# Moving HBM weight sums behind attention and retention, with a new issue order, in a hybrid decoder block

## The chip, the cores and the metric

The kernel runs on one core of a Trainium2 chip. The metric is the device time of one execution in microseconds, and lower is better. A core has TensorE (PE, matrix products and transposes), VectorE (DVE), ScalarE (ACT), GpSimd (POOL) and SyncE (SP). Every engine works through its own list of instructions in order, so an instruction that waits holds up all that stand behind it on that engine. SP issues nearly all loads and stores; POOL issues the transfers that add in HBM.

## The reference

One decoder layer, batch 1, 512 positions, width 1024, float32. The two mixers share one input projection; a gated sum of them goes through one output projection.

```python
h = rms_norm(x, norm_pre)
(q_n, k_c, v_c, k_s, v_s, k_w, v_w, g_n, z_n,
 q_r, k_r, v_r, z_r, m_a, m_b) = jnp.split(h @ w_in, split_points(), axis=-1)
# mixer A: 8 query heads of 64, 2 key groups; three branches, each with its own sigmoid gate
#   compressed keys (windows of 32, step 16, a two-layer gelu net), selected blocks, sliding window
o = g[..., 0:1] * o_c + g[..., 1:2] * o_s + g[..., 2:3] * o_w
y_a = (o * silu(z_n)) @ w_nsa_o
# mixer B: retention in chunks of 128, 4 heads, key width 128, value width 256
o_b = group_norm(o_inner + o_cross)
y_b = (o_b * silu(z_r)) @ w_ret_o
merged = sigmoid(m_a) * y_a + sigmoid(m_b) * y_b
x = x + rms_norm(merged @ w_out, norm_post)
```

With 512 positions the 16 "best" of 8 blocks are all blocks and the window covers every earlier position, so the selected and the sliding branch are both causal attention, on their own keys and values.

## The kernel before, in words

**Three products for one.** Each float32 matrix is held as a high part and a low remainder (hTh and hTl, whi and wlo), and a product is high x high + high x low + low x high, all summed in one PSUM bank (mm3). A weight tile comes by SP into one of NR = 4 raw buffers of 128x1024 words (512 KB); ACT or DVE copies it to the high part, DVE subtracts to get the low part (splitter, split_lo), and the parts lie in one of nine pairs of tiles until PE has used them. A few more pairs (more_tiles) come free in the course of the kernel; fits(p) says which pieces of weights may use them: MORE and MORE2 are ranges of load numbers.

**Stages.** PE's main line is in main(): first block A (attention keys and values, PE starts while h is still being made), C, Q; then the blocks of PLAN: Z (mixer A's output gate), MA0, ZR0, QK0, VR0, PAIR, VR1, MB0, NO0, RO0, MA1, NO1, MB1, RO1, and out_seven at the end. Z, MA and MB are the gates, QK, VR and ZR belong to retention (two halves of two heads), NO and RO are the two output matrices. Beside that line run the hidden layer of the compressed branch (hidden, its weights are 8 loads in the stream, HFIRST of which come ahead of Z's), 24 groups of attention (att_head, att_unit, att_block, att_cmp; att_sum ends one of the 8 pieces (t, g), in the order t = 3, 2, 1, 0) and 8 steps of retention (ret(hp, t), one per weight block row of VR).

**Seven products for eight.** PAIR, MA1, MB1 and out_seven are done as 2x2 block products with seven block products in place of eight (Strassen-Winograd's form). Such a product needs sums of blocks of its weights, and some of its inputs. The sums of weights are made in HBM: POOL issues 128x2048-word transfers (1 MB) that write a block to a scratch tensor, and others that add another block to it (accum_op=OP.add). The list seq has 8 transfers for PAIR (tensors pair, here p0 to p7), 8 for MA1 and MB1 together (t, s0 to s7), 8 for out_seven (out, o0 to o7), and three sums H0, H1, H2 of pieces of h (tensors s) that stand at the places HS of the list. In each group the first four write and the last four add. p4 needs p0, p5 needs p1, p6 needs p2 and p5, p7 needs p6 and p3; s and o are alike. H0, H1, H2 need the small stores of h by SP (signed). POOL waits for the landing of what a transfer needs before it issues it.

**Where the sums stand.** add_sums(n) issues the next n of the list. weight_sums issues FIRST = 8 once h is stored, and 27 - FIRST - sum(OSUMS) = 17 once the first tile of Z's gate is there (a POOL copy to a one-word tile named mark carries that wait). ret(hp, t) issues OSUMS[4*hp + t] more, right behind POOL's pow of that step. The finished sums are loaded by SP like other weights (load_next, the branch with DMA.dma_start(raw, o)); that load waits for the sum.

**The order of the work.** All these steps are generators. The class Order plays them at build time: it keeps a clock for PE and for each engine, yields give the time at which a step's input is ready, and of the steps that are ready (ready time + LAG + margin not after the clock) the one with the lowest priority number is issued next; with none, the earliest. PRIOS and MARGINS hold the priorities and the allowances (ns) by name of a generator, OWN those of single instances (split_lo.8 is the ninth split_lo that is spawned, which is the first of block C's). Order.dma models a load: a queue, 353 bytes per ns alone, slow (79 or 142) bytes per ns while a sum is in flight, and 1750 ns + BESIDE (if beside a sum) until it has landed. What comes out is only the order of the instructions on each engine; on the chip each waits for its true inputs.

**Others that the change touches.** EARLY_OUT lists the steps of retention whose PSUM bank is copied out by ACT before it is split. SKEW gives, for a block of weights, how many of its row pieces one output tile takes before the other tile of the pair takes its turn. HOLD_C is an allowance (ns) before the transposes of block C's keys.

Of the kernel before, what the change touches and what calls it, by code (L numbers as in the profile page):

```python
# [18 lines left out]
P = 128  # L19
# [16 lines left out]
MARGINS = {'att_cmp': 100.0, 'att_head': 150.0, 'att_out': 400.0, 'att_sum': 20.0, 'att_unit': 250.0, 'compress': 0.0, 'ga_split': 0.0, 'gates': 800.0, 'h_sums': 400.0, 'hidden': 800.0, 'keep': 0.0, 'kept': 1700.0, 'qk_end': 1700.0, 'ret': 20.0, 'ret_state': 150.0, 'rot_table': 400.0, 's_early': 50.0, 's_late': 150.0, 'seven_end': 0.0, 'split_lo': 150.0, 'splitter': 400.0, 'tail_a': 150.0, 'tail_c': 100.0, 'tail_m': 100.0, 'tail_o': 400.0, 'tail_p': 400.0, 'tail_q': 0.0, 'tail_qk': 600.0, 'tail_yb': 0.0, 'tail_z': 1300.0, 'x_split': 600.0, 'zr_end': 20.0}  # L36
# [7 lines left out]
HOLD_C = 1600  # L44
EARLY = 1300
HOLD = 2000
OSUMS = (1, 0, 0, 0, 1, 0, 0, 0)
FIRST, BESIDE = 8, 2500.0
HS = (4, 7, 9)
DVE_BIAS = 700  # L50
PRIOS = {'att_block': 0, 'att_cmp': 2, 'att_head': 3, 'att_out': 0, 'att_sum': 5, 'att_unit': 3, 'attention': 0, 'compress': 1, 'edges': 3, 'flip': 2, 'ga_split': 2, 'gates': 0, 'h_low': 1, 'h_split': 1, 'h_sums': 3, 'hidden': 3, 'keep': 5, 'kept': 0, 'more_tiles': 1, 'norms': 1, 'qk_end': 0, 'ret': 1, 'ret_state': 1, 'rot_table': 2, 's_early': 1, 's_late': 5, 'seven_end': 0, 'tail_a': 0, 'tail_c': 2, 'tail_m': 0, 'tail_o': 3, 'tail_p': 5, 'tail_q': 3, 'tail_qk': 0, 'tail_ya': 1, 'tail_yb': 3, 'tail_z': 0, 'tail_zr': 1, 'weight_sums': 0, 'x_split': 2, 'zr_end': 2}
OWN = {'edges.0': (5, 2200.0), 'gates.0': (None, 1700.0), 'h_low.0': (None, 100.0), 'h_low.4': (0, None), 'h_low.5': (None, 600.0), 'h_low.6': (1, None), 'more_tiles.0': (0, 150.0), 'norms.0': (None, 20.0), 'qk_end.2': (5, None), 'rot_table.5': (None, 2200.0), 'rot_table.6': (None, 250.0), 'signed.0': (2, 600.0), 'signed.1': (None, 0.0), 'signed.2': (0, 1300.0), 'signed.5': (None, 20.0), 'signed.7': (2, None), 'split_lo.0': (None, 800.0), 'split_lo.1': (None, 1000.0), 'split_lo.101': (4, None), 'split_lo.105': (1, None), 'split_lo.11': (3, None), 'split_lo.111': (None, 800.0), 'split_lo.13': (None, 600.0), 'split_lo.15': (2, 20.0), 'split_lo.19': (None, 400.0), 'split_lo.2': (0, None), 'split_lo.6': (2, None), 'split_lo.8': (4, 1300.0), 'split_lo.9': (None, 50.0), 'tail_a.0': (0, None), 'tail_a.2': (None, 400.0), 'tail_a.3': (0, 0.0), 'tail_c.1': (0, 20.0), 'tail_c.3': (1, None), 'tail_q.1': (1, 20.0), 'tail_qk.4': (None, 600.0), 'tail_qk.5': (None, 600.0), 'weight_sums.0': (0, 1000.0), 'x_split.0': (None, 20.0), 'zr_end.3': (1, None)}
HFIRST, HWANT = 1, 1
MORE, MORE2 = range(12, 24), range(24, 28)
EARLY_OUT = ((0, 3), (1, 0), (1, 3))
SKEW = {'Q': 4}
# [3 lines left out]
class Order:  # L60
# [47 lines left out]
    def dma(self, nbytes, r=0.0, n=1):  # L108
        for _ in range(n):
            self.ring = max(self.ring, r + LAG, self.flying.pop(0) + LAG) + 475  # L110
            t, left, beside = max(self.eng["dma"], self.ring + 100), nbytes / n, False
            slow = 79.0 if left <= P * 2048 else 142.0
            for i, (a, b) in enumerate(self.busy):
                if b <= t or left < 1:
                    continue
                free = min(left, max(0.0, a - t) * 353.0)
                left, t = left - free, t + free / 353.0
                if left >= 1:
                    part = min(left, (b - t) * slow)
                    left, t, beside = left - part, t + part / slow, True  # L120
# [2004 lines left out]
```

## Time and profile before

| | us |
|---|---|
| three runs | 483.2, 486.62, 487.13 |
| median | 486.62 |
| profiled execution, its own time | 486.01 |
| profiled execution, span of its instructions | 484.2 |
| PE busy in it | 469.9 (97%) |
| DVE, ACT, POOL busy in it | 410.4, 332.9, 37.7 |
| POOL's transfers (queue q0), share of 16 engines over the span | 22.8% |
| SP's transfers (queue q1), the same share | 43.2% |

The profiled execution's own time is 1.81 us above its span: that part lies outside the instructions. The median of the three runs is 0.61 us above the profiled one. A matmul's record is longer than the step from one to the next, because they are pipelined: the time between two starts is what one costs. Where a row says "<- ACT words L253", the instruction stood idle until that engine's instruction gave its signal. L301, L265, L253 and L278 are lines of helpers that many steps share, so the tiles' names tell what a row is: whi and wlo are split weights, arena_r holds keys, queries, values and block C's weights, bank is PSUM, words holds most float32 work, raw is a weight tile as it was loaded.

### The profile page before, as it was taken

The numbers are of one execution on the slowest core, as the hardware profiler recorded it, in microseconds if no ns is written. First come the engines' busy times: TensorE is split into PE (matmuls) and PEld (weight loads), VectorE is DVE, ScalarE is ACT, GpSimd is POOL, SyncE is SP. The second block draws the span as 40 slices with busy tenths as digits, with TensorE's granted clock in tenths as the row PEclk, the third lists the DMA queues.
The fourth block names the chain that finished last, engine by engine and source line by source line (L and its number), as shares of the span: only waits on it lengthen the run. The fifth ranks groups of instructions, "written<-read, shape, count | busy, mean of one in ns | idle before, by whom it ended". The sixth has DMA issues, their size and how long they took to land.

```text
span 484.2 us, 7839 instructions
## 1 busy us (share of the span) xinstructions
PE 469.9 (97%) x2676; PEld 419.7 (87%) x2676; DVE 410.4 (85%) x932; ACT 332.9 (69%) x717; POOL 37.7 (8%) x62
## 2 busy tenths in 40 slices
PE   8989999899999999999999999999999999999993
PEld 7879888788888888888989888998889989988882
DVE  5579899988898979889799998977776968989786
ACT  6787689679788899895687687765435435438742
POOL 2103020120002100000110001000000000000000
PEclk9999999999999999999999999999999999999997
DMA  8947999999968994125577662631474736626814
GB/s 307 398 139 252 352 324 272 292 275 396 286 149 199 361 190 129 68 85 177 111 231 263 216 207 83 134 128 40 141 256 151 226 102 200 222 100 214 249 70 164
DMA packets 31080, 98.75 MB, mean 204 GB/s; under 512 B 3136, under 2 KB 6976, under 8 KB 30272
## 3 DMA queue, kind: packets, MB, share of 16 engines
q1 hardware_dynamic: 24576, 70.85, 43.2%
q0 software_dynamic: 6320, 27.26, 22.8%
q8 instruction: 21, 0.34, 0.3%
q10 hardware_dynamic: 144, 0.14, 0.2%
q14 instruction: 19, 0.16, 0.1%
HBM read 93.52 MB, written 31.98 MB: 259 GB/s over the span
## 4 chain that ended last, share of the span: by engine, by line
PE 82%; DMA 6%; DVE 6%; ACT 5%; issue 1%; DVEq 0%; ACTq 0%; SPq 0%
PE bank L301 68%; PE bank L1342 8%; DMA raw<-in_stream_dram 4%; PE bank L307 4%; PE bank L1858 2%; ACT words L253 2%; DVE arena_r L265 2%; DVE words L265 2%; DMA words<-in_rope_r_dram 1%; DVE words L278 1%; ACT rsrow L253 1%; DMA words<-in_x_dram 1%; ACT whi L253 1%; ACT arena_r L253 1%; DVE wlo L265 1%
## 5 line engine op out<-in xcount | busy, mean ns | idle before, releaser
L253 ACT ACTIVATE whi<-raw 128x512 fp32r<-128x512 f32 x170 | 102.2, 627 | 47.5 <-PE bank L301 34.5
L265 DVE TENSOR_TENSOR wlo<-raw,whi 128x512 fp32r<-128x512 f32 x178 | 116.3, 686 | 6.4 <-ACT whi L253 4.8
L301 PE MATMUL bank<-whi,hTh 128*128 128x512 f32 x192 | 72.3, 398 | 1.2 <-ACT words L253 1.0
L301 PE MATMUL bank<-wlo,hTh 128*128 128x512 f32 x192 | 68.9, 379 | 0.0
L301 PE MATMUL bank<-whi,hTl 128*128 128x512 f32 x192 | 68.8, 379 | 0.0
L301 PE MATMUL bank<-arena_r 128*128 128x256 f32 (+2 forms) x328 | 66.6, 324 | 0.0
L301 PE MATMUL bank<-arena_r,whi 128*128 128x512 f32 (+1 forms) x208 | 61.4, 371 | 0.0
L253 ACT ACTIVATE arena_r<-bank 128x512 fp32r<-128x512 f32 (+3 forms) x86 | 45.6, 536 | 21.1 <-PE bank L307 20.5
L253 ACT ACTIVATE words<-words,stat 128x512 f32<-128x512 f32 (+3 forms) x108 | 56.6, 559 | 0.3 <-DVE stat L1071 0.2
L301 PEld LDWEIGHTS bank<-arena_r 128*128 128x128 f32 x328 | 50.9, 190 | 4.4 <-DVE arena_r L265 0.2
L265 DVE TENSOR_TENSOR arena_r<-bank,arena_r 128x512 fp32r<-128x512 f32 (+2 forms) x72 | 46.8, 655 | 5.8 <-ACT arena_r L253 5.1
L301 PEld LDWEIGHTS bank<-arena_r,whi 128*128 128x128 f32 x208 | 39.2, 189 | 5.0
L301 PE MATMUL bank<-hTh,whi 128*128 128x512 f32 (+1 forms) x124 | 43.1, 348 | 0.0
L301 PE MATMUL bank<-hTh,wlo 128*128 128x512 f32 (+1 forms) x124 | 42.0, 339 | 0.0
L301 PE MATMUL bank<-hTl,whi 128*128 128x512 f32 (+1 forms) x124 | 42.0, 339 | 0.0
L301 PEld LDWEIGHTS bank<-whi,hTh 128*128 128x128 f32 x192 | 36.7, 192 | 5.8 <-ACT words L253 1.5
L301 PEld LDWEIGHTS bank<-whi,hTl 128*128 128x128 f32 x192 | 36.4, 190 | 5.3
L301 PEld LDWEIGHTS bank<-wlo,hTh 128*128 128x128 f32 x192 | 36.4, 189 | 3.8
L307 PEld LDWEIGHTS bank<-identr,shorts 128*128 128x128 f32 x276 | 30.7, 141 | 7.9 <-ACT words L253 1.4
L301 PE MATMUL bank<-arena_r,wlo 128*128 128x512 f32 x96 | 36.4, 379 | 0.0
L253 ACT ACTIVATE words<-words 128x512 f32<-128x512 f32 (+3 forms) x47 | 27.4, 586 | 12.3 <-DVE words L265 5.6
L265 DVE TENSOR_TENSOR words<-bank,words 128x512 f32<-128x512 f32 (+3 forms) x56 | 33.8, 615 | 2.3 <-ACT rsrow L253 0.7
(195 smaller groups left out, 920.8 us busy)
## 6 DMA issues: line engine op xcount, KB each, us to landing
raw<-in_stream_dram SPq DMA_DIRECT2D x73, 512.0 KB, 4.6
pair<-in_stream_dram POOLq DMA_DIRECT2D x6, 1024.0 KB, 16.8
t<-in_stream_dram POOLq DMA_DIRECT2D x6, 1024.0 KB, 19.2
out<-in_stream_dram POOLq DMA_DIRECT2D x6, 1024.0 KB, 15.9
words<-in_x_dram SPq DMA_DIRECT2D x8, 512.0 KB, 7.8
raw<-s SPq DMA_DIRECT2D x8, 512.0 KB, 4.5
raw<-pair SPq DMA_DIRECT2D x8, 512.0 KB, 4.6
raw<-t SPq DMA_DIRECT2D x8, 512.0 KB, 4.4
```

Source lines behind the costliest of these rows:

```text
L253: S.activation(o, i, func, **kw)
L265: (V if e == "dve" else G).tensor_tensor(o, a, b, op=op)
L278: V.scalar_tensor_tensor(o, a, s, b, op0=op0, op1=op1)
L301: T.matmul(ps, a, b, start=start, stop=stop)
L307: T.transpose(ps, a, idn)
L1342: T.matmul(ps[m], a, apart(b), start=n in first and s + j == 0, stop=n in last and s + j == 5, skip_group_check=True)
L1858: T.matmul(ps[m], a, apart(b), start=n in first and s + i == 0, stop=n in last and s + i == 5, skip_group_check=True)
```

## The change

Eight of the sums that stood behind Z's gate go behind pieces of attention: ASUMS gives their number for the pieces in the order (3,0), (3,1), (2,0), (2,1), (1,0), (1,1), (0,0), (0,1). Four of the last group's go behind the four steps of retention's second half, where there had been one behind the first step of each half. 7 stay behind Z's gate in place of 17. In att_sum a POOL copy (to mark, over the 64 partitions of the piece) carries the wait for the piece, and no step issues before the flag "wsum", so the order of the list stays. H0 goes from place 4 to place 2 of the list (HS).

The model of a transfer in Order gets other figures, and it now knows that a load of a sum can't start before the sum has landed. MARGINS and PRIOS have other numbers in most of their entries, OWN is empty, HFIRST is 0 (Z's weights come ahead of all of the hidden layer's), MORE2 covers four loads more, EARLY_OUT has (0, 0) as well, SKEW has RO0 and RO1. No product, sum or split is added or taken away, but for one ACT copy in ret(0, 0).

```diff
--- before.py
+++ after.py
@@ -33,7 +33,7 @@
 LAG, PE_LAG = 55.0, 60.0
 TAIL = {"act": 110.0, "dve": 82.0, "pool": 45.0}
 MARGIN = 0.0
-MARGINS = {'att_cmp': 100.0, 'att_head': 150.0, 'att_out': 400.0, 'att_sum': 20.0, 'att_unit': 250.0, 'compress': 0.0, 'ga_split': 0.0, 'gates': 800.0, 'h_sums': 400.0, 'hidden': 800.0, 'keep': 0.0, 'kept': 1700.0, 'qk_end': 1700.0, 'ret': 20.0, 'ret_state': 150.0, 'rot_table': 400.0, 's_early': 50.0, 's_late': 150.0, 'seven_end': 0.0, 'split_lo': 150.0, 'splitter': 400.0, 'tail_a': 150.0, 'tail_c': 100.0, 'tail_m': 100.0, 'tail_o': 400.0, 'tail_p': 400.0, 'tail_q': 0.0, 'tail_qk': 600.0, 'tail_yb': 0.0, 'tail_z': 1300.0, 'x_split': 600.0, 'zr_end': 20.0}
+MARGINS = {'att_cmp': 100.0, 'att_head': 150.0, 'att_out': 150.0, 'att_sum': 250.0, 'att_unit': 400.0, 'compress': 20.0, 'ga_split': 0.0, 'gates': 1000.0, 'h_sums': 0.0, 'hidden': 0.0, 'keep': 400.0, 'kept': 250.0, 'qk_end': 50.0, 'ret': 20.0, 'ret_state': 50.0, 'rot_table': 1300.0, 's_early': 400.0, 's_late': 50.0, 'seven_end': 0.0, 'split_lo': 150.0, 'splitter': 400.0, 'tail_a': 150.0, 'tail_c': 50.0, 'tail_m': 20.0, 'tail_o': 600.0, 'tail_p': 600.0, 'tail_q': 1000.0, 'tail_qk': 600.0, 'tail_yb': 1000.0, 'tail_z': 1000.0, 'x_split': 20.0, 'zr_end': 100.0}
 SOON = 3
 PSOON = 8
 CSOON = 2
@@ -41,19 +41,20 @@
 SLACK = 700
 WAKE = 7
 SIGN, SIGN_LAG = 4, 25000.0
-HOLD_C = 1600
+HOLD_C = 500
 EARLY = 1300
 HOLD = 2000
-OSUMS = (1, 0, 0, 0, 1, 0, 0, 0)
-FIRST, BESIDE = 8, 2500.0
-HS = (4, 7, 9)
+OSUMS = (0, 0, 0, 0, 1, 1, 1, 1)
+ASUMS = (2, 2, 1, 1, 1, 1, 0, 0)
+FIRST, BESIDE = 8, 3200.0
+HS = (2, 7, 9)
 DVE_BIAS = 700
-PRIOS = {'att_block': 0, 'att_cmp': 2, 'att_head': 3, 'att_out': 0, 'att_sum': 5, 'att_unit': 3, 'attention': 0, 'compress': 1, 'edges': 3, 'flip': 2, 'ga_split': 2, 'gates': 0, 'h_low': 1, 'h_split': 1, 'h_sums': 3, 'hidden': 3, 'keep': 5, 'kept': 0, 'more_tiles': 1, 'norms': 1, 'qk_end': 0, 'ret': 1, 'ret_state': 1, 'rot_table': 2, 's_early': 1, 's_late': 5, 'seven_end': 0, 'tail_a': 0, 'tail_c': 2, 'tail_m': 0, 'tail_o': 3, 'tail_p': 5, 'tail_q': 3, 'tail_qk': 0, 'tail_ya': 1, 'tail_yb': 3, 'tail_z': 0, 'tail_zr': 1, 'weight_sums': 0, 'x_split': 2, 'zr_end': 2}
-OWN = {'edges.0': (5, 2200.0), 'gates.0': (None, 1700.0), 'h_low.0': (None, 100.0), 'h_low.4': (0, None), 'h_low.5': (None, 600.0), 'h_low.6': (1, None), 'more_tiles.0': (0, 150.0), 'norms.0': (None, 20.0), 'qk_end.2': (5, None), 'rot_table.5': (None, 2200.0), 'rot_table.6': (None, 250.0), 'signed.0': (2, 600.0), 'signed.1': (None, 0.0), 'signed.2': (0, 1300.0), 'signed.5': (None, 20.0), 'signed.7': (2, None), 'split_lo.0': (None, 800.0), 'split_lo.1': (None, 1000.0), 'split_lo.101': (4, None), 'split_lo.105': (1, None), 'split_lo.11': (3, None), 'split_lo.111': (None, 800.0), 'split_lo.13': (None, 600.0), 'split_lo.15': (2, 20.0), 'split_lo.19': (None, 400.0), 'split_lo.2': (0, None), 'split_lo.6': (2, None), 'split_lo.8': (4, 1300.0), 'split_lo.9': (None, 50.0), 'tail_a.0': (0, None), 'tail_a.2': (None, 400.0), 'tail_a.3': (0, 0.0), 'tail_c.1': (0, 20.0), 'tail_c.3': (1, None), 'tail_q.1': (1, 20.0), 'tail_qk.4': (None, 600.0), 'tail_qk.5': (None, 600.0), 'weight_sums.0': (0, 1000.0), 'x_split.0': (None, 20.0), 'zr_end.3': (1, None)}
-HFIRST, HWANT = 1, 1
-MORE, MORE2 = range(12, 24), range(24, 28)
-EARLY_OUT = ((0, 3), (1, 0), (1, 3))
-SKEW = {'Q': 4}
+PRIOS = {'att_block': 0, 'att_cmp': 2, 'att_head': 3, 'att_out': 5, 'att_sum': 5, 'att_unit': 3, 'attention': 2, 'compress': 2, 'edges': 2, 'flip': 3, 'ga_split': 2, 'gates': 5, 'h_low': 3, 'h_split': 3, 'h_sums': 3, 'hidden': 3, 'keep': 3, 'kept': 5, 'more_tiles': 2, 'norms': 2, 'qk_end': 0, 'ret': 1, 'ret_state': 1, 'rot_table': 2, 's_early': 2, 's_late': 5, 'seven_end': 0, 'tail_a': 0, 'tail_c': 2, 'tail_m': 2, 'tail_o': 0, 'tail_p': 5, 'tail_q': 3, 'tail_qk': 0, 'tail_ya': 5, 'tail_yb': 2, 'tail_z': 0, 'tail_zr': 1, 'weight_sums': 0, 'x_split': 2, 'zr_end': 2}
+OWN = {}
+HFIRST, HWANT = 0, 1
+MORE, MORE2 = range(12, 24), range(24, 32)
+EARLY_OUT = ((0, 0), (0, 3), (1, 0), (1, 3))
+SKEW = {'Q': 4, 'RO0': 4, 'RO1': 4}
 ROPES = ('dve', 'dve', 'dve')
 
 
@@ -109,19 +110,19 @@
         for _ in range(n):
             self.ring = max(self.ring, r + LAG, self.flying.pop(0) + LAG) + 475
             t, left, beside = max(self.eng["dma"], self.ring + 100), nbytes / n, False
-            slow = 79.0 if left <= P * 2048 else 142.0
+            slow = 70.0 if left <= P * 2048 else 125.0
             for i, (a, b) in enumerate(self.busy):
                 if b <= t or left < 1:
                     continue
-                free = min(left, max(0.0, a - t) * 353.0)
-                left, t = left - free, t + free / 353.0
+                free = min(left, max(0.0, a - t) * 350.0)
+                left, t = left - free, t + free / 350.0
                 if left >= 1:
                     part = min(left, (b - t) * slow)
                     left, t, beside = left - part, t + part / slow, True
                     for j in range(i, len(self.busy)):
-                        self.busy[j] = [self.busy[j][0] + part / 353.0 * (j > i), self.busy[j][1] + part / 353.0]
-            self.eng["dma"] = t = t + left / 353.0
-            self.flying.append(t + 1750 + BESIDE * beside)
+                        self.busy[j] = [self.busy[j][0] + part / 350.0 * (j > i), self.busy[j][1] + part / 350.0]
+            self.eng["dma"] = t = t + left / 350.0
+            self.flying.append(t + 2050 + BESIDE * beside)
         return self.flying[-1]
 
     def sums(self, e, ns):
@@ -457,7 +458,8 @@
         yield od.need("hq", "Z0")
         G.tensor_copy(mark, szn[:, 0, 0:1])
         od.op("pool", 70.0, zready[0])
-        add_sums(27 - FIRST - sum(OSUMS))
+        add_sums(27 - FIRST - sum(OSUMS) - sum(ASUMS))
+        od.flags.add("wsum")
 
     raws, parts, done = [], [], []
     WC = [tuple(at(44, 4480, FR)[:, (2 * p + i) * 560:(2 * p + i + 1) * 560] for i in range(2)) for p in range(KD // 2)]
@@ -494,6 +496,8 @@
                     o += P * n
                 else:
                     DMA.dma_start(raw, o)
+                    w = landed.get(o.tensor.name, 0.0)
+                    r = max(r, od.busy[w][1] + 1200 if isinstance(w, int) else w)
                 e = od.dma(P * n * 4, r)
                 c += n
                 if i + j == 0:
@@ -1177,6 +1181,12 @@
             for _ in range(2):
                 b = yield from PO.get()
                 PS.put(b)
+        n = ASUMS[2 * (NT - 1 - t) + g]
+        if n:
+            yield lambda: "wsum" in od.flags
+            G.tensor_copy(mark[m], gv[:, 0, 0:1])
+            od.op("pool", 70.0, e)
+            add_sums(n)
 
     ATT = tuple(f"att{t}{g}" for t in range(NT) for g in range(2))
```

## The prediction, on record before the result

> **What bounds the kernel now.** I read the page first, then busy time by stages, who waits for whom on PE, and the transfers by stretch.
>
> ```profile
> span 484.2 us, 7839 instructions
> PE 469.9 (97%) x2676; PEld 419.7 (87%) x2676; DVE 410.4 (85%) x932; ACT 332.9 (69%) x717; POOL 37.7 (8%) x62
> q0 software_dynamic: 6320, 27.26, 22.8%
> ```
>
> (q0 is POOL's transfers: packets, MB, share of 16 engines.) PE leaves 484.2 - 469.9 = 14.3 us of the span free. The question is where. The next rows are the stages: length, busy time of PE, PEld, DVE, ACT and POOL, then granted clock, DMA share and GB/s.
>
> ```profile
> 20.00:100.00 80.00, 75.93 (x467) 67.37 (x467) 69.43 (x190) 60.89 (x139) 12.97 (x20) 1.00 0.92 277
> 100.00:130.00 30.00, 29.94 (x172) 26.04 (x172) 27.60 (x71) 25.39 (x58) 5.89 (x7) 1.00 1.03 331
> 130.00:470.00 340.00, 339.52 (x1935) 305.06 (x1934) 290.14 (x629) 229.24 (x489) 15.29 (x18) 1.00 0.57 170
> 470.00:484.20 14.20, 5.80 (x27) 4.72 (x25) 9.92 (x22) 3.30 (x10) 0.00 (x0) 0.78 0.40 148
> ```
>
> PE is idle for 4.07 us in 20-100, 0.06 in 100-130, 0.48 in 130-470 and 8.40 at the end; the remaining 1.3 us lie in the first 20. So from 20 to 470 a perfect order could win 4.07 + 0.06 + 0.48 = 4.61 us by the records, 0.95% of the time. The records hide a little more, since a pipelined matmul's record reaches over the next start. The chain of waits shows how much:
>
> ```profile
> 5.00 21.25 PE bank L301 x93
> 271.66 9.07 PE bank L1342 x42
> ```
>
> 42 matmuls of 512 columns in PAIR take 9.07 us, 216 ns each; the 93 of block A take 228 ns each, so 93 x 12.5 ns = 1.2 us are lost there that no idle time shows. The clock was granted in full in both stages. This is a kernel at its PE bound with about 6 us to be had before its tail, and much more to be lost.
>
> **The transfers.** The first rows are POOL's, in order of time, then SP's loads in three stretches (median us from issue to landing).
>
> ```profile
> 45.75 2.98 POOL L446 DMA_DIRECT2D pair<-in_stream_dram  x4
> 62.09 1.17 POOL L444 DMA_DIRECT2D s<-s  x1 [13.37 <-DMA s<-words]
> 62.81 2.83 POOL L444 DMA_DIRECT2D pair<-in_stream_dram  x2
> 86.42 0.51 POOL L458 COPY mark<-words 128x1 f32<-128x1 f32 x1 [10.89 <-DVE words L278]
> 101.44 3.02 POOL L446 DMA_DIRECT2D t<-in_stream_dram  x4
> 116.83 1.15 POOL L444 DMA_DIRECT2D t<-in_stream_dram  x1 [12.37 <-DMA t<-in_stream_dram]
> 150.34 3.00 POOL L446 DMA_DIRECT2D out<-in_stream_dram  x4
> ```
>
> ```profile
> raw<-in_stream_dram SPq DMA_DIRECT2D x10, 512.0 KB, 11.5
> ```
>
> ```profile
> raw<-in_stream_dram SPq DMA_DIRECT2D x6, 512.0 KB, 9.7
> ```
>
> ```profile
> raw<-in_stream_dram SPq DMA_DIRECT2D x6, 512.0 KB, 3.5
> out<-out POOLq DMA_DIRECT2D x1, 1024.0 KB, 8.2
> ```
>
> These are the stretches 62-100 (first), 100-130 (second) and 300-340 (last two). A load beside sums takes some three times as long as one with hardly any. Yet in 100-130, where the DMA share is over 1, PE was idle for 0.06 us: the loads run ahead. A load is two row pieces of 12 matmuls each, 24 x 216 ns = 5.2 us of PE; with four raw buffers in turn a landing time of up to about 20 us is covered.
>
> **The change part by part.**
>
> *Eight sums from behind Z to behind attention, two more to retention.* s4 stood at 116.8 and o0 at 150.3; the last four adds for the output are o4 to o7, which the 17 behind Z and two steps of retention issued. The pieces of attention end at DVE's gate products:
>
> ```profile
> 161.07 1.38 DVE L265 TENSOR_TENSOR words<-words,words 64x512 f32<-64x512 f32 x2
> 206.85 1.46 DVE L265 TENSOR_TENSOR words<-words,words 64x512 f32<-64x512 f32 x3
> ```
>
> So s4 to s7 move to about 161 and after, o0 to o3 to about 167-208, and o4 to o7 to the four steps of VR1, at about 301, 310, 325 and 334:
>
> ```profile
> 300.89 0.70 POOL L265 TENSOR_TENSOR rv<-rv,nhalf 128x2 f32<-128x2 f32 x1 [25.62 <-DVE rv L272]
> 334.01 1.00 POOL L265 TENSOR_TENSOR rv<-rv,nhalf 128x2 f32<-128x2 f32 x1 [8.62 <-DVE rv L272]
> 355.48 14.37 SPq L496 DMA_DIRECT2D raw<-t  x4
> 417.04 2.74 SPq L496 DMA_DIRECT2D raw<-out  x2
> ```
>
> The sums t are first loaded at 355 and out at 417. Four adds in a row from 161, at the 8.2 us of the add above or double that, end by 225 at the latest; o7, issued at 334, lands by 350. No load waits for a sum: 0 us, with 67 us or more of cover. POOL's queue: behind each sum that waits stand the later sums and, in VR1, the pow of the next step, for which ACT's scaling waits. o6 must wait for o5 (issued 310.5, landing by 327) and the next pow is at 334: 7 us of cover, 0 us. The six added POOL copies cost 6 x 0.51 = 3.1 us on an engine that is busy for 8%.
>
> What does it win? Sums leave 117-160 and loads there land sooner; PE waits for none of them there: between 0 and 0.5 us, the idle time of 100-470. I take 0.1.
>
> The nearest rows for what a POOL copy costs DVE are the copy at 86.42 and DVE's work beside it, against the mean of such work:
>
> ```profile
> 86.20 0.68 DVE L265 TENSOR_TENSOR shorts<-raw,shorts 128x512 fp32r<-128x512 f32 x1
> 86.80 1.29 DVE L265 TENSOR_TENSOR wlo<-raw,whi 128x512 fp32r<-128x512 f32 x2
> ```
>
> ```profile
> L265 DVE TENSOR_TENSOR wlo<-raw,whi 128x512 fp32r<-128x512 f32 x178 | 116.3, 686 | 6.4 <-ACT whi L253 4.8 <-PE bank L307 0.7
> ```
>
> 0.68 us beside the copy and 0.69 on the mean: 0 us. [...]
>
> *H0 before p2.* H0 waits for h's stores: POOL stood for 13.37 us until 62.09. p2 and p3, issued ahead of it so far, now stand behind it and p4, p5 behind them. Two plain transfers move from 46-62 into 62-100. One of them takes 22.8% of 484.2 = 110.4 us over 27.26 MB, 4.05 us per MB or 4.25 us of all 16 engines, so 8.5 us of transfer work move into a stretch that is full. Against it, the stores and loads of 46-62 land sooner and H0 with them. Bounds: -0.5 us (PE's recorded wait at 57.6 goes, below) and +8.5 us (all of it reaches PE). I take 0: 11.5 us of landing may grow to 16 or so and stays within 20.
>
> *The new order, block C.* PE's two longest recorded waits are alike:
>
> ```profile
> PE bank L301 <- ACT words L253: 1.9, 3, 1.0
> PE bank L301 <- DVE arena_r L265: 1.9, 2, 1.0
> ```
>
> ```profile
> 27.78 0.56 DVE L770 COPY words<-words 128x768 f32<-128x768 f32 x1
> 28.36 0.37 DVE L265 TENSOR_TENSOR arena_r<-words,arena_r 128x64 fp32r<-128x64 f32 x2
> 28.64 0.73 DVE L265 TENSOR_TENSOR arena_r<-raw,arena_r 128x560 fp32r<-128x560 f32 x1
> 29.43 0.39 PE L301 MATMUL bank<-arena_r,hTh 128*128 128x280 f32 x1 [1.00 <-DVE arena_r L265]
> ```
>
> DVE did the doubled keys (0.56) and two value splits (0.37) of block A's tail ahead of a low part of C's weights (0.73) for which PE stood 1.00 us. OWN had set split_lo.8 back (priority 4, 1300 ns) and split_lo.11 too (3); without OWN they go by rank, 0 when PE is near. Of the 1.9 us I take half, -1.0, bounds -1.9 and +1.4: h_low falls from priority 1 to 3, and where two weight splits go ahead of it, PE waits for two of DVE's 0.7 us.
>
> *The rest of the order.* The other 1.9 us are copies that ACT did late, at these places:
>
> ```profile
> 57.65 0.48 PE L301 MATMUL bank<-whi,hTh 128*128 128x512 f32 x1 [0.47 <-ACT words L253]
> ```
>
> ```profile
> 90.22 0.38 PE L301 MATMUL bank<-whi,arena_r 128*128 128x256 f32 x1 [0.99 <-ACT words L253]
> ```
>
> ```profile
> 292.58 0.48 PE L301 MATMUL bank<-whi,hTh 128*128 128x512 f32 x1 [0.48 <-ACT words L253]
> ```
>
> Smaller allowances (hidden 800 to 0, kept 1700 to 250, qk_end 1700 to 50) let PE's list take a step closer to its input; larger figures for loads beside sums (landing 2050 + 3200 ns for 1750 + 2500, 125 for 142 bytes per ns) put others later. By the new figures a 512 KB load beside a sum takes 4.2 + 5.3 = 9.4 us, by the old 3.7 + 4.3 = 7.9; the medians above are 9.7 and 11.5, so the new ones are nearer. I take half of the 1.9 us, -0.9; bounds -1.9 and +6.4 (below).
>
> HFIRST, MORE2, SKEW and EARLY_OUT add no matmul. EARLY_OUT's one more ACT copy costs 0.7 us on an engine at 69%: nothing on PE. HOLD_C and the tail of 8.4 us: 0, bounds -1 and +1, since the chain behind PE's last product is the same.
>
> Sum: 0.1 + 1.0 + 0.9 = 2.0 us less; against the profiled execution 486.0 - 2.0 = 484.0. The median is 0.6 above that execution: **484.6 us**, 0.4% less.
>
> **The rivals.**
>
> *The transfers were hidden anyway, and the order trades one wait for another.* For it: 0.06 us of idle time in 100-130. It gives 486.6 us.
>
> *The order closes nearly every gap.* Idle 4.61, the 1.2 of block A, and 0.8 off the 8.40 of the tail (an estimate: one DVE step such as the 0.73 above): 6.6 us, 480.0 us. For it: the model is nearer to the trace where waits are. Against: 4.07 of the 4.61 lie in 20-100, where DVE is busy for 69.43 of 80 us and the sums for PAIR stay.
>
> *Slower: the loads starve in 62-100.* H0's place pushes p2 to p5 into Q, Z and the hidden layer. The price is the 8.5 us, less about 2 that the time ahead of it gives back (the DMA share is 0.92 over 20-100, so 6.4 us of transfer time are free there in all, of which I count a third as lying ahead, an estimate): 6.5 us, 493.1 us. It decides once loads take over 20 us, as the four buffers are then all in flight. Against: it needs nearly a doubling.
>
> *Slower: steps are placed before their inputs are there.* Attention, PAIR and retention hand over between PE, ACT and DVE step by step, and smaller allowances bite where the model is early. Each such wait costs 0.5 to 1.0 us by the rows above; eight of them 0.8 each are 6.4 us, 493.0 us. Against: from 130 to 470 the old order, with its own misses, lost 0.48 us.
>
> **How the numbers follow.** About 1% (4.9 us) is what a measurement of this kernel can tell from no change; its three runs span 0.8%. My forecast, a gain of up to 4 us: 0.34. Hidden anyway: 0.20. Every gap closed: 0.18. Loads starve: 0.11. Steps too early: 0.17. Half of each slower case's neighbourhood lies near the 1% line, and I count it as slower: faster 0.18, within 1% 0.54, slower 0.28. The range leaves out a little on both sides: from 479.5 (just under the closed gaps) to 493.5 (just over both slower cases). The likeliest case's own range is 482.5 to 486.5.
>
> **What would show it.** Right: POOL's rows show s4 to o3 between about 161 and 210, o4 to o7 behind the pows of VR1; loads in 100-130 land in well under 9.7 us, PE's idle time there is still near zero; the two waits of 1.0 us for arena_r near 28-31 shrink. Starving would show as PE idle time in 62-100 above 3 us, with splits on ACT waiting for raw, and landing over 20 us. Steps too early would show as new rows PE <- ACT or PE <- DVE behind 130, and idle time there far above 0.48 us. A time under 480 would mean that more was hidden behind the records than I counted.

## The result, and the profile after

The changed kernel takes 481.83 us (median of 15 runs, 481.51 to 485.61), beside 484.51 us for the kernel before (15 runs, 483.2 to 487.27): a ratio of 0.9945, 95% interval 0.9923 to 0.9966. On a second chip it took 481.83 us again, beside 486.32 us: 0.9915 (0.9894 to 0.9937). By these ratios it is 2.7 to 4.1 us faster. The forecast was 484.6 us, with 479.5 to 493.5 as its range; 481.83 lies in the range, and 0.7 us under the likeliest case's own (482.5 to 486.5). Of the 2.8 us between 484.6 and 481.83, 2.1 are the kernel before, whose median is 484.51 us in these 15 runs and was 486.62 in the three that the forecast started from. The profiled execution took 481.54 us, 4.5 us less than the one profiled before.

The top of the page after, then its stages (length, busy time of PE, PEld, DVE, ACT and POOL, granted clock, DMA share, GB/s):

```profile
span 479.8 us, 7856 instructions
PE 468.1 (98%) x2676; PEld 418.9 (87%) x2676; DVE 411.0 (86%) x936; ACT 331.8 (69%) x714; POOL 39.5 (8%) x68
```

```profile
20.00:100.00 80.00, 77.47 (x483) 69.42 (x481) 72.47 (x199) 62.99 (x145) 13.22 (x20) 1.00 0.91 281
100.00:130.00 30.00, 30.00 (x175) 26.50 (x173) 25.53 (x67) 21.63 (x49) 3.68 (x5) 1.00 0.98 326
130.00:470.00 340.00, 338.52 (x1926) 303.86 (x1926) 294.18 (x635) 230.51 (x493) 18.83 (x26) 1.00 0.57 172
470.00:479.80 9.80, 3.36 (x16) 2.61 (x14) 5.61 (x13) 2.31 (x8) 0.00 (x0) 0.94 0.30 107
```

PE's idle time fell from 4.07 to 2.53 us in 20-100 and from 8.40 to 9.80 - 3.36 = 6.44 us at the end; it rose from 0.48 to 1.48 us in 130-470. That is 2.5 us of the 4.4 us by which the span fell. Block A gave 0.8 more (not from the change, as the last section shows); 1.1 us lie at the start and in steps between matmuls, which no idle time shows.

The chain of waits goes through PE nearly from end to end now (93% of the span by the page), and block A's 93 matmuls stand in it with 20.43 us where they had 21.25:

```profile
4.77 20.43 PE bank L302 x93
...
437.10 36.27 PE bank L1868 x168
```

The waits that the forecast meant to halve, as PE's waits and as the rows of DVE ahead of the first:

```profile
PE bank L302 <- DVE arena_r L266: 1.9, 2, 1.0
PE bank L302 <- ACT words L254: 1.7, 3, 0.8
```

```profile
26.73 0.56 DVE L774 COPY words<-words 128x768 f32<-128x768 f32 x1
27.31 0.37 DVE L266 TENSOR_TENSOR arena_r<-words,arena_r 128x64 fp32r<-128x64 f32 x2
27.60 0.73 DVE L266 TENSOR_TENSOR arena_r<-raw,arena_r 128x560 fp32r<-128x560 f32 x1
```

```profile
28.39 0.39 PE L302 MATMUL bank<-arena_r,hTh 128*128 128x280 f32 x1 [1.00 <-DVE arena_r L266]
30.50 0.39 PE L302 MATMUL bank<-arena_r,hTh 128*128 128x280 f32 x1 [0.94 <-DVE arena_r L266]
...
221.42 0.48 PE L302 MATMUL bank<-whi,hTh 128*128 128x512 f32 x1 [0.78 <-ACT words L254]
```

DVE still does the doubled keys and two value splits ahead of block C's low part: the same three pieces with the same lengths. Of the three waits behind ACT, the one of 0.99 us at 90.22 is gone, and one of 0.78 us at 221.42 is new.

POOL's transfers (copies and pows left out; start, time, what, and the idle time before it):

```profile
44.66 1.64 POOL L447 DMA_DIRECT2D pair<-in_stream_dram  x2
57.30 1.17 POOL L445 DMA_DIRECT2D s<-s  x1 [11.00 <-DMA raw<-in_stream_dram]
58.01 1.83 POOL L447 DMA_DIRECT2D pair<-in_stream_dram  x2
59.37 1.68 POOL L445 DMA_DIRECT2D pair<-in_stream_dram  x1
...
103.26 3.12 POOL L447 DMA_DIRECT2D t<-in_stream_dram  x4
```

```profile
145.49 2.32 POOL L445 DMA_DIRECT2D t<-in_stream_dram  x2 [0.73 <-issue]
...
211.35 0.68 POOL L447 DMA_DIRECT2D out<-in_stream_dram  x1
...
299.12 1.20 POOL L445 DMA_DIRECT2D out<-in_stream_dram  x1
...
332.56 0.86 POOL L445 DMA_DIRECT2D out<-out  x1
```

The sums stand where the diff puts them: s4 to o3 from 145 to 211, o4 to o7 behind the pows from 299 to 333. H0 is issued at 57.30 in place of 62.09.

### The profile page after: what moved, and what is told of

It is laid out like the page before. It is cut to its first block, busy times and chain, and to the rows that moved or that the text cites. A ratio compares the mean times of both kernels' runs of the same rounds, so it can differ in the third digit from the quotient of the medians.

```text
span 479.8 us, 7856 instructions
## 1 busy us (share of the span) xinstructions
PE 468.1 (98%) x2676; PEld 418.9 (87%) x2676; DVE 411.0 (86%) x936; ACT 331.8 (69%) x714; POOL 39.5 (8%) x68
## 4 chain that ended last, share of the span: by engine, by line
PE 93%; ACT 3%; DVE 2%; DMA 1%; issue 0%; DVEq 0%; ACTq 0%
PE bank L302 74%; PE bank L1352 8%; PE bank L1868 8%; PE bank L308 4%; ACT words L254 2%; ACT arena_r L254 1%; DMA words<-in_x_dram 1%; DVE arena_r L266 1%; DVE words L266 0%; ACT shorts L254 0%; DVE words L279 0%; DVE words L1075 0%; ACT rsrow L254 0%; ACT whi L254 0%; DVE words L774 0%
## 5 line engine op out<-in xcount | busy, mean ns | idle before, releaser
L266 DVE TENSOR_TENSOR wlo<-raw,whi 128x512 fp32r<-128x512 f32 x182 | 119.2, 686 | 8.0 <-ACT whi L254 7.3
L302 PE MATMUL bank<-arena_r 128*128 128x256 f32 (+2 forms) x328 | 65.4, 322 | 0.0
L254 ACT ACTIVATE words<-words,stat 128x128 f32<-128x128 f32 (+3 forms) x109 | 56.7, 553 | 1.9 <-DVE stat L266 1.1
L302 PE MATMUL bank<-hTh,whi 128*128 128x512 f32 (+1 forms) x120 | 41.4, 345 | 0.0
L302 PE MATMUL bank<-hTl,whi 128*128 128x512 f32 (+1 forms) x120 | 40.5, 337 | 0.0
L302 PE MATMUL bank<-hTh,wlo 128*128 128x512 f32 (+1 forms) x120 | 40.5, 337 | 0.0
```

The lines of the kernel that those rows point to most:

```text
L254: S.activation(o, i, func, **kw)
L266: (V if e == "dve" else G).tensor_tensor(o, a, b, op=op)
L302: T.matmul(ps, a, b, start=start, stop=stop)
```

## The experiments

In the kernels whose names begin with x1, x3, x5, x6 and x7, only POOL's transfers (and the copies that carry their waits) are moved: the order's model still plays the sums at the places of the kernel that each starts from, so that PE, DVE, ACT and SP keep their instructions in the same order. They ran on three chips; each ratio is to the kernel before on the same chip.

| kernel | us (lowest to highest) | ratio, 95% | before beside it |
|---|---|---|---|
| x1_before_new_sums | 484.49 (482.1-486.26) | 0.997 (0.9945-0.9994) | 486.08 |
| x2_before_x_last | 485.03 (482.76-486.75) | 0.9986 (0.9962-1.001) | 486.08 |
| x3_after_old_sums | 484.86 (483.68-486.84) | 0.9981 (0.9954-1.0007) | 486.08 |
| e5_after_old_figures | 491.2 (490.5-493.09) | 1.0121 (1.0087-1.0154) | 486.08 |
| x5_before_h0 | 483.56 (482.27-487.54) | 0.9948 (0.9921-0.9976) | 486.54 |
| x6_before_att_sums | 486.23 (485.25-489.15) | 1.0007 (0.9984-1.003) | 486.54 |
| x7_after_sums_from_z | 481.84 (481.63-485.73) | 0.9913 (0.9882-0.9943) | 486.54 |
| f1_after_landing_1750 | 487.63 (485.56-488.41) | 1.0022 (0.9999-1.0044) | 486.54 |
| a1_after_again | 481.83 (481.62-482.6) | 0.9915 (0.9894-0.9937) | 486.32 |
| x8_after_c_early | 481.23 (480.96-482.01) | 0.9904 (0.988-0.9927) | 486.32 |
| x9_after_both | 481.64 (481.04-486.63) | 0.9916 (0.9889-0.9943) | 486.32 |
| e8_after_old_tables | 490.38 (487.92-490.85) | 1.0076 (1.0049-1.0104) | 486.32 |

### The sums' places alone, and the order alone

x1 is the kernel before with every sum at its new place; x3 is the kernel after with every sum at its old place.

```diff
+    for i, h in zip((2, 7, 9), hsums):
+        rseq[i:i] = [(*h, True)]
...
         add_sums(27 - FIRST - sum(OSUMS))
+        real(27 - FIRST - sum(RSUMS) - sum(ASUMS))
+        od.flags.add("wsum")
...
+        n = ASUMS[2 * (NT - 1 - t) + g]
+        if n:
...
+            G.tensor_copy(mark[m], gv[:, 0, 0:1])
+            real(n)
```

(x1; real(n) issues the next n of rseq, add_sums only tells the model. In x3 rseq has (4, 7, 9), RSUMS is the old OSUMS, and the copies behind attention are left out.)

> The kernel before, with its order of instructions on PE, DVE, ACT and SP kept row for row; POOL alone issues the sums of weights at the new places (7 behind Z's gate, 8 behind pieces of attention, 4 behind VR1, H0 ahead of p2). Theory: the sums' place wins almost nothing by itself, since PE waited for no load in 100-160; ratio to the kernel before 0.998 to 1.001, and loads in 100-130 land in some 8 us for 9.7. Rival, the sums' place is the gain: ratio near 0.9945, the whole of the change.

> The changed kernel, its order on PE, DVE, ACT and SP kept row for row; POOL alone issues the sums at the old places (17 behind Z's gate, one behind the first step of each half of retention, H0 behind p3). Theory: no more than 0.5 us is lost; ratio to the kernel before 0.9945 to 0.996. Rival, the sums' place is the gain: ratio near 1.000, and PE idle time in 80-180 up by 2 us or more.

The places give 0.3% in the old order (1.5 us by the ratio, interval 0.3 to 2.7). The new order with the old places gives 0.2% (0.9 us, interval from 2.2 us faster to 0.3 slower). x1 gained a little more than was expected of it, and x3 lost far more: with the old places most of the gain is gone, near its rival's 1.000 (PE's idle time rose in 62-100, by 1.2 us, and not in 80-180 as that rival had it). In the new order the places are worth 0.4 to 0.7% (x3's ratio against the two of the change), 1.7 to 3.2 us, measured on different chips. By the medians neither alone gives what the two give together; the intervals of x1 and of the change's first ratio overlap.

### Which of the places

x5 is the kernel before with H0 alone moved ahead of p2 and p3. x6 is the kernel before with all new places but that one.

```diff
+    rseq = list(seq)
+    for i, h in zip((2, 7, 9), hsums):
+        rseq[i:i] = [(*h, True)]
...
         add_sums(FIRST)
+        real(FIRST)
...
```

(x5. In x6 it is (4, 7, 9), with ASUMS and RSUMS as in x1.)

> The kernel before, its order kept row for row on every engine, but for one swap on POOL: H0 stands ahead of p2 and p3. Theory: this swap is what the sums' place wins; with two transfers in flight for four in 45-62 the loads land in 7 to 10 us for 11.6, less is queued up at 62, and PE's idle time in 62-100 falls from 1.7 us to near 0.7. Ratio to the kernel before 0.9955 to 0.998. Rival, the gain is in the sums behind attention: ratio 0.999 to 1.001.

> The kernel before, its order kept on PE, DVE, ACT and SP, with the sums behind attention and VR1 as in the change, but H0 behind p3 as before. Theory: nothing is won, since PE waited for no load behind 100: ratio to the kernel before 0.999 to 1.001, PE's idle time in 62-100 stays at 1.7 us or more. Rival: ratio 0.9955 to 0.998.

The intervals don't meet, so in the old order this is settled: H0's place gives 0.5% (2.5 us, interval 1.2 to 3.8) and the ten sums that leave Z's gate give nothing (1.0007). The two ran on one chip, 2.7 us apart. x5's ratio is as low as the first one of the whole change (0.9945), but its median is 1.7 us above the change's.

The profiles show how in part. Where H0 is behind p3, as in x6, PE is idle for 1.3 us or more in 62-100; where it is ahead, for 0.64 us or less in the kernels of the table, with one exception (x5):

```profile
62.00:100.00 38.00, 35.08 (x206) 30.16 (x205) 33.48 (x76) 29.25 (x60) 6.59 (x7) 1.00 1.05 286
```

| PE idle in 62-100, us | H0 behind p3 | H0 ahead of p2 |
|---|---|---|
| old order | 1.67 (before), 2.81 (x2), 2.92 (x6) | 0.64 (x1), 2.02 (x5) |
| new order | 1.34 (x3) | 0.12 (after), 0.13 (a1), 0.12 (x7), 0.15 (x8) |

(A profile is one execution. x5's took 487.54 us, the longest of its twelve, so it doesn't show what x5's median gained; x1's, 482.1 us, was the shortest of twelve, and x2's, 486.75 us, the longest. So the old order's row is weak evidence. In the new order's row x7's was the longest of eight, 485.73 us, and shows 0.12 all the same.) What PE waited for is seen in the chain of waits that leads to 130 us: its shares by line in 60-130, first before, then x6 and after.

```profile
by line: PE bank L301 40.4%; DMA raw<-in_stream_dram 18.2%; ACT words L253 12.3%; DMA words<-in_rope_r_dram 7.6%; PE bank L307 6.1%; ACT whi L253 4.5%; DVE arena_r L265 3.1%; issue 2.8%; DVE wlo L265 2.7%; ACT arena_r L253 1.1%; DVE shorts 
```

```profile
by line: PE bank L303 49.0%; DMA raw<-in_stream_dram 39.8%; PE bank L309 5.6%; DVE wlo L267 2.7%; issue 2.1%; ACT whi L255 0.9%; ACT words L255 0.5%; DVE gate L276 0.3%; ACT shorts L255 0.1%; ACTq L255 0.1%
```

```profile
by line: PE bank L302 85.4%; PE bank L308 7.9%; ACT words L254 3.7%; ACT arena_r L254 1.3%; issue 1.0%; ACT whi L254 0.9%
```

In the first two weight loads carry 18 and 40% of that chain (in x3 22%); in the kernel after they carry none. But H0's move alone doesn't take the loads off it: in the old order they carry 31% in x1 and 45.5% in x5. What differs there with H0's place is how fast the loads issued in 45-62 land: in 7.3 us (x1) and 7.1 us (x5), against 11.6, 12.7 and 13.0 us (before, x2, x6). Those of 62-100 land no sooner: 10.4 and 12.1 us, against 11.5, 12.1 and 10.3. x6 shows the pieces of such a chain:

```profile
60.96 14.04 DMA raw<-in_stream_dram
...
75.68 1.31 DVE wlo L267 x2
...
77.00 13.85 DMA raw<-in_stream_dram
...
90.96 0.07 ACT shorts L255
...
91.50 0.38 ACT words L255
...
91.92 0.92 PE bank L303 x4
```

A load of 14.04 us, its split, the next load into a raw buffer that this set free for 13.85 us, and then the copy by ACT for which PE stands, queued behind a split that waited for that load. So a landing time of 14 us is not covered here.

### The transfers made still lighter

x7 is the kernel after with no sum ahead of Z's gate: 11 transfers behind it, and 4, 4, 1, 1, 1, 1 behind the pieces of attention.

```diff
+RASUMS = (4, 4, 1, 1, 1, 1, 0, 0)
...
+        real(11)
         od.flags.add("wsum")
```

> The changed kernel, its order kept on PE, DVE, ACT and SP; POOL issues no sum ahead of Z's gate, 11 behind it (p0 to p7 and H0 to H2), 4 and 4 behind the first two pieces of attention, the rest as changed. If transfers in 45-85 are what PE pays for in 62-100, this wins more: loads there land in 5 us or less, idle time in 62-100 near 0, ratio to the kernel before 0.991 to 0.994 (the change itself: 0.9945). Rival, the rest of that idle time has other causes, or the sums for PAIR come too late (raw<-pair waits at 217-260): ratio 0.9945 or more.

The loads of 62-100 land in 4.3 us where they took 8.9 in the kernel after, and nothing comes of it: 481.84 us, and 0.12 us of PE idle in that stretch, as in the kernel after. Its ratio of 0.9913 lies where more gain was expected, but the changed kernel itself has 0.9915 on another chip. Here, with the loads off the chain already, lighter transfers are worth nothing.

### The tail

x2 is the kernel before with the two loads of x issued behind the last weight load in place of ahead of it.

```diff
+            if i == len(loads) - 1:
...
+                for t in range(2):
+                    DMA.dma_start(at(30 + 4 * t, D), x[t * P:(t + 1) * P, :])
...
             for t in range(2):
-                DMA.dma_start(at(30 + 4 * t, D), x[t * P:(t + 1) * P, :])
                 od.dma(P * 4096, max(s4r))
```

> The kernel before, one thing moved: the two loads of x that stood between the last two loads of weights stand behind both; all else row for row the same. Theory: the tail's 2.0 us (8.4 us from PE's last product to the end before, 6.4 after the change) come from the last weights' landing, 7.0 us beside the loads of x; ratio 0.996 (2 us less), the tail near 6.4 us. Rival, the tail's gain has another cause (DVE's order in the last stage): ratio 1.000, tail 8.4 us.

In the kernel before, the chain leaves PE at 451.21 and runs through the last weight load and then through DVE and ACT to the end; in x2 it is PE until the last product, as it is in the kernel after (437.10, above). Before, then x2:

```profile
439.54 11.67 PE bank L1858 x54
451.21 1.06 ACT words L253 x2
...
453.54 6.98 DMA raw<-in_stream_dram
```

```profile
442.07 33.68 PE bank L1862 x156
```

SP's rows show that the new order made the same swap (before, then after):

```profile
448.67 5.20 SPq L496 DMA_DIRECT2D raw<-in_stream_dram  x3
453.92 0.90 SPq L1739 DMA_DIRECT2D words<-in_x_dram  x2
455.30 0.33 SPq L496 DMA_DIRECT2D raw<-in_stream_dram  x1
```

```profile
445.93 7.36 SPq L498 DMA_DIRECT2D raw<-in_stream_dram  x4
453.33 0.99 SPq L1749 DMA_DIRECT2D words<-in_x_dram  x2
```

PE's idle time from 470 to the end is 8.40, 6.62, 7.34 and 7.72 us in four profiles with the old place of the x loads (before, x1, x6, x5) and 6.3 to 6.7 us in ten with the new one (x2, after and all others): 1.1 us less on the mean, though x1's 6.62 with the old place is no more than some of these. The timing of x2 (0.9986, for 0.996 expected) agrees with 0.7 us but doesn't exclude zero. That is about what x3, the new order with the old sums, gained (0.9 us).

### The model's figures and the tables

e5 is the kernel after with the old figures in the model of transfers; f1 changes one of them back, the landing time; e8 has the new figures, but the old MARGINS, PRIOS and OWN. In all three every sum stays at its new place.

```diff
-FIRST, BESIDE = 8, 3200.0
+FIRST, BESIDE = 8, 2500.0
...
-            slow = 70.0 if left <= P * 2048 else 125.0
+            slow = 79.0 if left <= P * 2048 else 142.0
...
-            self.flying.append(t + 2050 + BESIDE * beside)
+            self.flying.append(t + 1750 + BESIDE * beside)
```

(e5, which also has 353 for 350 and leaves out the two lines on landed sums; no run took those two lines out alone. f1 has the last pair alone.)

> The changed kernel with the old figures in the model of a transfer, and without the model's knowledge that a load of a sum waits for the sum; tables, sums and all else as changed, the order comes out anew. Theory: the figures matter where loads run beside sums, in 45-130; with the old ones PE idle time in 20-100 goes from 2.5 back towards 4 us: ratio to the kernel before 0.997 to 1.001. Rival, the figures only shuffle the order: ratio 0.992 to 0.997, PE idle time in 20-100 near 2.5.

> The changed kernel with one of the five figures as it was: 1750 ns until a load has landed in place of 2050; the order comes out anew (172 rows of PE's list differ). Theory, nearer figures make a better order step by step: a small loss, ratio to the kernel before 0.995 to 0.998, lost where loads run beside sums (45-130). Rival, any other figure gives just another order: a ratio anywhere from 0.988 to 1.012, the difference in stretches where loads don't limit, as in 200-240 with all the old figures.

> The changed kernel with the old MARGINS, PRIOS and OWN; figures, sums and the small switches as changed, the order comes out anew. If tables and figures belong together and any mismatch gives just another order: a ratio to the kernel before of 1.00 to 1.015, lost at hand-overs between engines behind 130, as with the old figures. If the figures and the sums' place carry the gain whatever the tables: 0.993 to 0.997.

All three are slower than the kernel after, by 9.4, 5.8 and 8.6 us against its 481.83; e5 lies outside both ranges that were written down for it, f1 in its rival's, e8 in its first. Little of it lies in 62-100, where loads count (PE idle for 0.86, 0.00 and 0.51 us). PE's longest waits in e5, f1 and e8:

```profile
220.00 0.79 PE L302 MATMUL bank<-arena_r 128*128 128x512 f32 x1 [2.88 <-DVE arena_r L266]
```

```profile
339.92 0.54 PE L308 MATMUL bank<-identr,shorts 128*128 128x128 f32 x4 [2.42 <-ACT words L254]
```

```profile
216.37 0.48 PE L302 MATMUL bank<-whi,hTh 128*128 128x512 f32 x1 [3.12 <-DVE words L266]
```

They are hand-overs of attention and retention behind 130 (e8's product of weights waits for attention's step on DVE), which is what the rival of steps placed too early described. In f1 ACT's scaling ahead of that wait stood behind the last pow of VR1, at 337.92 where the kernel after has it at 331.58. So these runs don't show that figures nearer to the trace give a better order by themselves: the loss lies where loads don't limit. They agree with tables and figures that fit each other only as a set, but three orders that were worse don't prove it; that the changed order is simply a good one among many was not tested.

### Block C

x8 goes after the two waits of 1.0 us: the low part of C's third weight row comes right behind its high part on DVE, and the fourth row is split earlier on ACT and DVE.

```diff
...
+                if KD <= p < 14:
+                    V.tensor_tensor(vl, src, f(vh), op=OP.subtract)
+                if p == 12:
...
+                    (h4, l4), s4 = WC[3], raws[i + 1][0][:, 0:560]
+                    S.activation(h4[:, 0:560], s4, AF.Copy)
+                    low4.append(lambda: V.tensor_tensor(l4[:, 0:560], s4, f(h4[:, 0:560]), op=OP.subtract))
...
         e = doubled(kn, 0, 384, kd, e)
+        if low4:
+            low4.pop()()
```

> The changed kernel once more, beside the next runs on one chip, since the kernel before scatters by several us from chip to chip. Expected: 481.5 to 482.6 us in most runs, ratio to the kernel before 0.991 to 0.9945. The last study's kernel with no sum ahead of Z came to 481.84 us on another chip, the change to 481.83: on one chip the two differ by less than 0.1%.

> The changed kernel, its order kept but for block C's last two weight tiles: the low part of the third stands right behind its high part on DVE, the fourth's high part goes two places up on ACT and its low part ahead of the first value splits on DVE. Theory: PE's two waits of 1.0 us for arena_r near 28-31 shrink to 0.5 us in all, and PE's list keeps what it wins: 1.5 us less, ratio to the changed kernel 0.997. Rival, DVE is the bound there (72 of 80 us busy in 20-100), so the tail of block A comes later by as much and PE waits for it behind: ratio 0.999 to 1.001.

> Block C's tiles early, as in the run before this, and no sum ahead of Z's gate as well. Theory: the two are apart in time and add up, but the second wins nothing in most runs: the same as the run before this within 0.1%. If it is below it by more, sums in 45-85 still cost something in the changed kernel.

In x8 the first wait shrinks to 0.22 us, the second goes, and two others come (PE's rows from 27 to 34):

```profile
28.32 0.39 PE L302 MATMUL bank<-arena_r,hTh 128*128 128x280 f32 x1 [0.22 <-DVE arena_r L582]
29.78 0.37 PE L308 MATMUL bank<-identr,shorts 128*128 128x128 f32 x2 [0.24 <-DVE words L783]
32.79 0.54 PE L308 MATMUL bank<-shorts,shorts 128*128 128x128 f32 x4 [0.78 <-DVE arena_r L266]
```

1.94 us become 1.24: 0.7 us, and 481.23 us against the 481.83 of the same kernel without the edit on the same chip is 0.6, where 1.5 was expected. It is the fastest version that ran, but the two intervals overlap, so it is not settled that it beats the changed kernel. x9, with x7's places as well, adds nothing to it (481.64).

## Why the prediction was right or wrong

The size of the change was forecast nearly right (a gain below 1%), but in good part by luck: most terms of the sum behind it were wrong, and their errors happened to cancel. The terms, in their own order:

**Sums behind attention: 0.1 us.** Right. x6 measures nothing (from 0.8 us faster to 1.5 slower), and no load waits for a sum. POOL's copies show no cost either: the six take 0.18 to 0.64 us each, and DVE's 512-wide steps that run beside them 0.67 to 0.69 us (1.29 for two), where DVE's low parts took 0.69 on the mean before. Loads in 100-130 land in 8.0 us for 9.7, less of a fall than "well under 9.7" meant, and PE was idle for 0.06 us there to begin with.

**H0 ahead of p2: "I take 0", -0.5 to +8.5.** Wrong, and outside its bounds; it is the main gain, 1.5 us (x1, with the other places) to 2.5 us (x5) in the old order. The step that failed is the cover: "a load is two row pieces of 12 matmuls each, 24 x 216 ns = 5.2 us", times four buffers. In 62-100 many of the loads are the hidden layer's. Their products have 256 columns, and there are only two (high and low part), not three, for each block:

```profile
83.06 0.27 PE L301 MATMUL bank<-whi,arena_r 128*128 128x256 f32 x1
83.17 0.28 PE L301 MATMUL bank<-wlo,arena_r 128*128 128x256 f32 x1
```

One follows another in 0.11 us. The profile before has 64 of them (22 on whi, 22 on wlo and 20 on a pair named shorts), 60 of these in 62-100, for the 8 loads of the hidden layer. So such a load has 8 products, 8 x 0.11 = 0.9 us of PE, a sixth of what I counted, and a raw buffer is held until DVE's split of it is done. That this is what shortens the cover is argued from these rows; no run changed the hidden layer's loads. But landing times of 11.5 us there were already on the chain that sets PE, which the row of 18.2% above would have told, had I asked for the chain of that stretch and not of the end alone. I priced only the work that H0's move pushes into 62-100. That it takes work out of 45-62, where the loads that feed 62-100 are in flight, I bounded with one recorded wait. In the kernel after, loads of 45-62 land in 9.7 us for 11.6 and those of 62-100 in 8.9 for 11.5.

**Block C: -1.0 us.** Wrong: the waits are unchanged (1.9 us). The step that failed is that an empty OWN sets the low parts forward. DVE's three pieces come in the same order without it, and with the old OWN, MARGINS and PRIOS (e8) the two waits are 1.9 us as well. A priority only chooses among steps that are ready, which may be why; no run took that apart. When x8 split the tiles earlier, the two waits' 1.9 us gave 0.6.

**ACT's copies: -0.9 us.** By the records 0.2 us (1.9 to 1.7). The 0.99 us wait at 90.22 went, mostly with the new order: 0.16 us of it is left in x3 (new order, old sums), 0.64 in x1 and 1.20 in x5 and x6 (old order). The step that failed is that nothing comes in place of what goes: a wait of 0.78 us at 221.42 is new.

**Tail: 0.** Wrong by the profiles: 2.0 us in the two, about 1.1 on the means above; x2's timing gives 0.7 and doesn't exclude zero. "The chain behind PE's last product is the same" is true, but in the kernel before PE's last product was not on the chain: a late weight load was, and the new order issues it ahead of the x loads. I had moved no load in my sum but those of the diff's lists; a new order moves loads too.

**Block A's 1.2 us.** Not lost by the order, as the rival of closed gaps had it: see the last section.

So 2.0 us were forecast from the wrong places. What the runs show is 1.5 to 2.5 us from H0 in the old order and, by the profiles, about 1.1 us from the tail, less 1.0 us of new waits in 130-235: 1.6 to 2.6 us, against 2.7 to 4.1 measured. The rest may be what the new order and H0's place give only together in 62-100, where PE's idle time fell to 0.1 us with both. That the places are worth 1.7 to 3.2 us in the new order (x3) agrees with this, but no run moved H0 alone there. Of the rivals, starving loads turned out the other way round: the swap relieves the loads of 45-62, and those of 62-100 land no later. Long hand-overs, as in the rival of steps placed too early, are what e5, f1 and e8 show, but the changed kernel itself has only 1.0 us of it.

What stays open: how much of the gain is the new order's at all (x3's interval includes none), why loads left the chain only with both the new order and H0's place, and whether x8 is faster than the change.

## What to carry to other kernels

Before a transfer is called hidden, follow the chain of waits to the end of that stretch, not to the end of the kernel; a DMA row there says that the landing time counts, even where PE's recorded waits name only ACT or DVE. Work out a buffer's cover from the smallest work that PE gets out of a load in that stretch, and look at when each load is issued as well as at how long it takes. An issue order found for one set of costs need not be worth anything for another (three such mismatches lost 5.8 to 9.4 us here): a change to a model's figure has to be timed as a change of the whole order.

## What the runs showed of the hardware

**Half rate around some waits.** In e5 the mean granted clock was 1.00 in 210-218 and 0.51 in 218-225, the stretch in which its wait of 2.88 us ends (at 220.00). In x9 it was 1.00 in 195-203 and 0.57 in 203-211, behind a wait of 2.20 us (until 202.80). In x7 it was 0.57 in 33-37, behind no more than block C's two waits (1.9 us in all, the second until 33.02); in before and after the same two waits, 1.9 us in all, are followed by a clock of 1.00 in 33-37. The three stretches, e5, x9 and x7:

```profile
218.00:225.00 7.00, 5.00 (x13) 4.01 (x14) 6.17 (x12) 1.45 (x4) 0.68 (x2) 0.51 0.93 309
```

```profile
203.00:211.00 8.00, 8.00 (x34) 6.88 (x34) 7.14 (x24) 4.92 (x16) 0.00 (x0) 0.57 0.13 38
```

```profile
33.00:37.00 4.00, 3.98 (x20) 3.98 (x21) 3.78 (x16) 4.00 (x13) 0.49 (x1) 0.57 0.81 240
```

In e5's stretch matmuls of 512 columns follow each other in 0.43 us (222.20 to 222.63) in place of 0.216. Over the 5.00 us that PE was busy there I estimate 2.5 us from that, beside the 2.88 of the wait. Yet f1's wait of 2.42 us (until 339.92) was followed by a clock of 1.00 in 340-347. So the length of a wait alone doesn't tell here whether half rate follows; what decides it was not shown.

**Block A's first matmuls are slower in some executions.** PE's matmuls in 5 to 7 us, before and after:

```profile
5.00:7.00 2.00, 2.00 (x5) 1.64 (x6) 1.94 (x5) 1.22 (x3) 0.00 (x0) 1.00 1.01 361
```

```profile
5.00:7.00 2.00, 2.00 (x10) 1.50 (x10) 1.73 (x5) 1.32 (x3) 0.00 (x0) 1.00 0.95 345
```

PE is busy throughout in both, with 5 starts in one and 10 in the other, though the clock's column says 1.00 in both. The first four take 1.87 us before (5.00 to 6.87, 0.47 us each) and 0.97 us after (4.77 to 5.74, 0.24 each); four later ones take 0.86 (7.73 to 8.59) and 0.87 us (7.54 to 8.41). In x7 the first eight take 3.58 us (5.19 to 8.77) and the next four 1.30. It isn't the change: the same kernel run again (a1) had 5 starts in 5-7, and the old order (x1) had 9. Block A's 93 matmuls take 21.25 us before, 20.43 after and 22.54 in x7. In the profile before, the first four alone cost 1.0 us more than 4 x 0.216; that is most of the 1.2 us which I had put down to the order. The two effects go a long way to explain a long execution: x7's profiled one took 3.9 us more than its median, and against the profile after it lost 2.1 us in block A (22.54 for 20.43) and, with a clock of 0.57 over the 4 us behind block C, about 1.7 us more (0.43 x 4, an estimate).
